# A hybrid encoder on one core: the first pair of up tiles as eight plain half products, with its combinations of activations made during it

## The chip, the core and the metric

The kernel runs on one core of a Trainium2 chip. The core has five engines with a queue of instructions each: PE (TensorE) multiplies matrices, DVE (VectorE), ACT (ScalarE) and POOL (GpSimd) work element by element, SP (SyncE) here issues nearly all DMAs. They run side by side and wait for each other by semaphores. PE's results go to PSUM, which this kernel uses as eight banks of 128 x 512 f32 values; the tiles named below lie in SBUF, the other on-chip memory.

The metric is the device time of one execution in microseconds (us). A run gives one such time; the median of several runs is compared.

## The reference, cut to what matters

One encoder layer is applied to 1024 prompt tokens and 256 sample tokens. The part that the change touches is the end of the cross-attention and the beginning of the feed-forward network:

```python
x = x + memory_cross_attention(rmsnorm(x, norm_xa_w), rmsnorm(mem, norm_mem_w), xa_w_q, xa_w_kv, xa_w_o)
h = rmsnorm(x, norm_ffn_w)
gu = h @ ffn_w_gate_up
x = x + (jax.nn.silu(gu[..., :D_FF]) * gu[..., D_FF:]) @ ffn_w_down
```

D_MODEL is 1024 and D_FF is 2816, so h @ ffn_w_gate_up has 22 gate tiles and 22 up tiles of 128 columns. Tile f of each belong together: silu(gate) * up is one row block of the input of the down product.

## The kernel before

**Precision.** Every f32 operand x of a matrix product is split into two parts, hi (x rounded by a copy on ACT) and lo = x - hi (on DVE or POOL), and a product is three matmuls: hi by hi, lo by hi, hi by lo (`mm3`). `split` makes both parts, and its lo part always has the line L126, the hi part L125. All matmuls of PE that matter here have the line L108.

**Tiling.** Activations lie transposed: 128 partitions of the model dimension, tokens along the free axis, eight such tiles (k = 0 to 7) for 1024. The tokens are in three blocks: x0 (prompt, 512), x1 (prompt, 512) and x2 (sample, 256). A weight tile has 128 x 1024 values: eight k pieces of 128 x 128.

**The up stage** (`ff_first`, `ff_up`, driven by `up`) runs over f = 0 to 21, one gate tile and one up tile per f; here such an f is called a pair. For the prompt, the pair's gate and up tile (two columns of blocks) by the two halves of the model dimension (k 0 to 3 and k 4 to 7) by the two token blocks are a 2 x 2 by 2 x 2 block product, done with seven half products rather than eight, each of 4 k pieces, 12 matmuls of 512 columns. It needs sums of the weight tiles (`gu_sa`, `gu_sb`, on POOL, in the tile `room`) and combinations of the activations, which are made once: b11 and b21 are the two halves of x0's normed activations, b12 and b22 those of x1's, r1 = b11 - b12, r2 = b22 - r1 (up to sign), t3 = b22 - b12, t4 from r2 and b21. r1 lies in the place of b12. The sample's products are plain (`sample`): 24 matmuls of 256 columns each for gate and up.

**Before it** the output projection of the attention (`OutProj.run`) computes x0, x1, x2 (evacuated by DVE, L1230) and starts three norms (`Norm.rest`) as side jobs: x0's, x1's and the sample's. A norm sums squares, has a step on PE (matmul of nacc by a column of ones), a chain of eleven short DVE instructions (L258, L224, L226 to L228) for the inverse root nst, a second step on PE (nst by the identity), then for each k a multiplication on DVE (L276) and a split. In the kernel before, x1's norm makes r1 in x0 (L1422) and r2 in four banks of PSUM (`r2_raw`, L1426) as it goes; `make_t3` (L1559) and `make_t4` (L1568) follow in `ff_first` between the seven products of the first pair.

**What sets the order.** PE's order is the order in which the Python code emits its instructions: the main generator (`K.main`) emits products, and after each one the side jobs whose time has come by an estimated clock (`K.clock`, `pump`) emit theirs; LAGS, LAGS2 and PACE1 are such delays. The order on the other engines is made by a scheduler when the program is built. Each engine then executes its queue strictly in order. PSUM's banks are two pools of four: pm for the products of the main generator, pq (`bank()`) for the norms, sums and the sample.

**Loads.** `gu_load` loads the pair f's two weight tiles by SP, alternately into two places; `gu_gate`, `gu_sa`, `gu_sb`, `gu_up` split them, with the lo parts mostly on POOL. For the first pair, `first_weights` and `after` do so during the output projection. Results of the up stage go to DRAM (gq for the prompt's combinations, gsd for the sample); the down stage after it is not touched.

Of the kernel before, what the change touches and what calls it, by code (L numbers as in the profile page):

```python
# [163 lines left out]
def trunk_kernel(ctx: ExitStack, tc: tile.TileContext, a):  # L164
# [52 lines left out]
    def bank(p=pq, tag="b"):  # L217
        return p.tile([P, 512], F32, tag=tag, name="bank")
# [1195 lines left out]
    def sinks(b, x, hs):  # L1414
        hi, lo = hs[b]
        x0, x1 = x[0], x[1]
        if b == 0:
            return lambda k, t: split(hi[:, k, :], lo[:, k, :], t, V if k % 2 else G)

        def sink(k, t):  # L1420
            if k < 4:
                V.tensor_tensor(out=x0[:, k, :], in0=x0[:, k, :], in1=t, op=ALU.subtract)  # L1422
                split(hi[:, k, :], lo[:, k, :], x0[:, k, :], V)
            else:
                r2_raw.append(bank())
                V.scalar_tensor_tensor(out=r2_raw[k - 4], in0=t, scalar=-1.0, in1=x0[:, k - 4, :], op0=ALU.mult, op1=ALU.subtract)  # L1426
# [6 lines left out]
    r2_raw = []  # L1433
    first_out = []

    def copies_read():

        if not first_out:
            return False
        h3[2] = h3[2][0], hp.tile([P, KT, NS], F32R, tag="lo2", name="lo2")  # L1440
        return True
# [48 lines left out]
    def first_weights():  # L1490

        gu_load(0, wp)

        def sums():
            yield FIRST_W
            g, u = gu_raw[0]
            hi, lo = gu_w[0, 1] = pair_of(wp)
            s2, s1 = bank(), bank()
            V.tensor_tensor(out=s1, in0=u[:, :512], in1=u[:, 512:], op=ALU.add)
            V.tensor_tensor(out=s2, in0=s1, in1=g[:, :512], op=ALU.add)  # L1500
            gu_gate(0)
            split(hi[:, :512], lo[:, :512], s2)
            split(hi[:, 512:], lo[:, 512:], s1)
            yield 3000
            V.tensor_tensor(out=g[:, :512], in0=g[:, :512], in1=u[:, :512], op=ALU.add)
            V.tensor_tensor(out=g[:, 512:], in0=s2, in1=g[:, 512:], op=ALU.add)

        K.side(sums())
# [30 lines left out]
    def parts(hl, k, src, eng):  # L1539
        split(hl[0][:, k, :], hl[1][:, k, :], src, eng)  # L1540

    def r2_ready():
        for k in range(4):
            parts(r2, k, r2_raw[k], V)

    K.main(op.run(x1d, 1.0, S_FFN, x2p, x2d, sinks, first_weights, copies_read, after))
    x0, x1 = op.x[0], op.x[1]
    K.finish(K.pending.pop((id(h3), 1)))
# [3 lines left out]
    first_copies = hp.tile([P, 4, 512], F32, tag="lo2", name="copies")  # L1552
    split(*gu_w[0, 3], gu_raw[0][1], G)
    fs = ExitStack()
    t4 = []

    def make_t3():
        for k in range(4):
            V.tensor_tensor(out=x1[:, k, :], in0=x1[:, k + 4, :], in1=x1[:, k, :], op=ALU.subtract)  # L1559
            parts(t3, k, x1[:, k, :], V)  # L1560
        xhs.close()

    def make_t4():
        nonlocal fp
        fp = fs.enter_context(pool("ffn", side="right"))
        t4.extend(fp.tile([P, 4, 512], F32R, tag=f"t4{i}", name=f"t4{i}") for i in "hl")
        for k in range(4):
            V.scalar_tensor_tensor(out=x0[:, k + 4, :], in0=r2_raw[k], scalar=-1.0, in1=x0[:, k + 4, :], op0=ALU.mult, op1=ALU.subtract)  # L1568
            parts(t4, k, x0[:, k + 4, :], V)

    def make_room():
        nonlocal room
        room = x0p.tile([P, KT, 512], F32, tag="x0", name="room")

    fp = room = None
# [153 lines left out]
    def ff_first():  # L1729


        w = lambda i: gu_w[0, i]
        pb, pf, pe, pa = (bank(pm) for _ in range(4))
        cs = first_copies
        gu_load(1, wp)
        yield from gu_mm(pb, w(0), 1, b21, True)
        yield from gu_mm(pa, w(0), 0, b11, True)
        p1 = copied(pa, cs[:, 0, :])
        t1 = gate_of(pb, p1)
        yield from gu_mm(pe, w(1), 1, r1, True)  # L1740
        make_t3()
        yield from gu_mm(pa, w(1), 0, r2, False)
        gu_gate(1, V)
        yield from gu_mm(pf, w(2), 1, b22, True)
        u2 = copied(pa, cs[:, 1, :])
        V.tensor_tensor(out=u2, in0=u2, in1=pe, op=ALU.add)
        t2 = gate_of(pf, u2)
        make_t4()
        make_room()
        yield from gu_mm(pa, w(2), 0, t3, False)  # L1750
        c22 = copied(pa, second_block(0))
        V.tensor_tensor(out=c22, in0=c22, in1=pe, op=ALU.add)
        times_up(t2, c22, store2(0), -1.0, c22)
        pn = bank(pm)
        yield from gu_mm(pn, gu_w[1, 0], 0, b11, True)
        yield from gu_mm(pa, w(3), 1, t4, False)
        times_up(t1, pa, store1(0), -1.0)
        pending["last"] = 0, t1, c22
        pn2 = bank(pm)
        first_out.extend((pn, pn2))  # L1760
        yield from gu_mm(pn2, gu_w[1, 0], 1, b21, True)

    def ff_up(f):
        w = lambda i: gu_w[f, i]
        second, last = f == 1, f == NFF - 1
        sums = lambda: (bank()[:, :NS], bank()[:, :NS])
        if second:
            pa, pb = first_out
            p1 = copied(pa)
            t1 = gate_of(pb, p1)  # L1770
            combine(*pending["last"])
            K.finish(K.pending.pop((id(h3), 2)))
            smp.extend(half(h3[2], i) for i in range(2))
            sg0, su0 = sums()
            yield from sample(sg0, gu_w[0, 0], (0, 1))
            gu_sa(1)
            ts0 = silu2(sg0, NS)
            sg, su = sums()
            yield from sample(su0, gu_w[0, 3], (0, 1))
            times_up(ts0, su0, gsd[0], 1.0)  # L1780
        else:
            pa, pb = bank(pm), bank(pm)
            yield from gu_mm(pa, w(0), 0, b11, True)
            p1 = copied(pa)
            sg, su = sums()
            yield from sample(sg, w(0), (0,))
            yield from gu_mm(pb, w(0), 1, b21, True)
            t1 = gate_of(pb, p1)
            combine(*pending["last"])
        gu_sb(f)  # L1790
        gu_load(f + 1, wp if f % 2 == 0 else x2p)
        yield from sample(sg, w(0), (0, 1) if second else (1,))
        yield from gu_mm(pa, w(1), 0, r2, False)
        u2 = copied(pa)
        gu_up(f)
# [9 lines left out]
        yield from sample(su, w(3), (0, 1))  # L1805
# [248 lines left out]
LAGS, LAGS2, FIRST_W = 11000, 9000, 9000  # L2054
PACE1 = 1900
# [82 lines left out]
```

## Time and profile before

| | us |
|---|---|
| median of 3 runs | 2257.51 |
| all runs | 2257.51, 2257.01, 2261.9 |
| span of the profiled execution | 2255.3 |
| busy in it: PE / DVE / ACT / POOL | 2197.5 / 1394.5 / 816.5 / 536.0 |
| the up stage in it begins | 1396.98 |

The profiled execution is another one than those timed, and its own time is known by its span, from the first to the last instruction; what lies around it is the difference to a run's time, some 2 us against the median.

How to read the views that follow: a line of the timeline has the start, the duration, the engine, the line of the kernel, the operation, its output and input by the program's names, the shape, and a count where equal instructions follow each other; in brackets stands how long the engine was idle before it and what ended that. Matmuls overlap in the pipeline, so the step from start to start is the price of one, and not its duration. In a view of windows the columns are the window, its length, the busy time of PE, PE's weight loads, DVE, ACT and POOL (with counts), then the granted clock of PE, the busy share of the DMA engines and GB/s. Line numbers (L1568) are those of the kernel printed above.

### The profile page before, as it was taken

The numbers are of one execution on the slowest core, as the hardware profiler recorded it, in microseconds if no ns is written. First come the engines' busy times: TensorE is split into PE (matmuls) and PEld (weight loads), VectorE is DVE, ScalarE is ACT, GpSimd is POOL, SyncE is SP. The second block draws the span as 40 slices with busy tenths as digits, with TensorE's granted clock in tenths as the row PEclk, the third lists the DMA queues.
The fourth block names the chain that finished last, engine by engine and source line by source line (L and its number), as shares of the span: only waits on it lengthen the run. The fifth ranks groups of instructions, "written<-read, shape, count | busy, mean of one in ns | idle before, by whom it ended". The sixth has DMA issues, their size and how long they took to land.

```text
span 2255.3 us, 32407 instructions
## 1 busy us (share of the span) xinstructions
PE 2197.5 (97%) x12464; PEld 1919.1 (85%) x12464; DVE 1394.5 (62%) x2765; ACT 816.5 (36%) x1480; POOL 536.0 (24%) x361
## 2 busy tenths in 40 slices
PE   6999999999999999999999998999999999999998
PEld 6988888888888898788888887888888888878888
DVE  7768788887985964664533547543443344468575
ACT  5434243433424433232344423332323232343453
POOL 3010000000000000013221332656665666100031
PEclk9999999999999999999999999999999999999999
DMA  5222322323234445962231432222222222493531
GB/s 186 83 79 68 104 69 87 79 66 95 73 115 121 159 142 166 310 226 94 91 101 43 164 135 74 81 90 84 83 84 79 78 86 96 152 338 108 201 108 57
DMA packets 191302, 262.48 MB, mean 116 GB/s; under 512 B 72410, under 2 KB 102698, under 8 KB 191146
## 3 DMA queue, kind: packets, MB, share of 16 engines
q1 hardware_dynamic: 171306, 231.30, 30.5%
q10 hardware_dynamic: 19840, 29.11, 3.5%
q8 instruction: 98, 1.61, 0.3%
q14 instruction: 58, 0.48, 0.1%
HBM read 182.19 MB, written 78.16 MB: 115 GB/s over the span
## 4 chain that ended last, share of the span: by engine, by line
PE 83%; DVE 8%; issue 4%; DMA 3%; ACT 2%; POOL 0%; SPq 0%; POOLq 0%; ACTq 0%; DVEq 0%
PE bank L108 82%; DMA tbd<-stage 1%; PE bank L121 1%; DVE acc L591 1%; DVE wlo L126 1%; DMA braw<-gq 1%; DVE nt L276 1%; DVE lo L126 0%; DVE sw L895 0%; DVE U L837 0%; DMA t<-sgd 0%; DVE nacc L244 0%; DVE aT L706 0%; ACT acc L589 0%; ACT whi L125 0%
## 5 line engine op out<-in xcount | busy, mean ns | idle before, releaser
L108 PE MATMUL bank<-hi,whi 128*128 128x512 f32 (+1 forms) x2144 | 762.8, 356 | 0.0
L108 PE MATMUL bank<-lo,whi 128*128 128x512 f32 (+1 forms) x2144 | 748.1, 349 | 0.0
L108 PE MATMUL bank<-hi,wlo 128*128 128x512 f32 (+1 forms) x2144 | 747.8, 349 | 0.0
L108 PEld LDWEIGHTS bank<-hi,wlo 128*128 128x128 f32 x2144 | 405.4, 189 | 53.9
L108 PEld LDWEIGHTS bank<-hi,whi 128*128 128x128 f32 x2144 | 406.2, 189 | 49.4 <-issue 0.2
L108 PEld LDWEIGHTS bank<-lo,whi 128*128 128x128 f32 x2144 | 406.4, 190 | 48.4 <-issue 0.2
L126 POOL TENSOR_TENSOR wlo<-raw,whi 128x1024 fp32r<-128x1024 f32 x72 | 174.0, 2418 | 467.2 <-ACT whi L125 467.2
L125 ACT ACTIVATE whi<-raw 128x1024 fp32r<-128x1024 f32 (+1 forms) x135 | 140.5, 1042 | 241.0 <-PE bank L108 182.7
L108 PE MATMUL bank<-bhl,whi 128*128 128x512 f32 x456 | 140.5, 389 | 0.0
L126 POOL TENSOR_TENSOR wlo<-room,whi 128x1024 fp32r<-128x1024 f32 x42 | 100.8, 2401 | 51.9 <-ACT whi L125 50.8
L108 PEld LDWEIGHTS bank<-bhl,whi 128*128 128x128 f32 x456 | 85.5, 188 | 17.8
L126 DVE TENSOR_TENSOR wlo<-raw,whi 128x1024 fp32r<-128x1024 f32 (+1 forms) x63 | 75.4, 1197 | 31.3 <-ACT whi L125 28.7
L1802 DVE TENSOR_TENSOR room<-room,bank 128x512 f32<-128x512 f32 x21 | 14.5, 688 | 127.0 <-ACT room L1588 127.0
L108 PE MATMUL bank<-bhl,wlo 128*128 128x512 f32 x228 | 88.8, 390 | 1.7 <-DVE wlo L126 1.7
L591 DVE SCALAR_TENSOR_TENSOR acc<-craw,sm,acc 128x510 f32<-128x510 f32 (+1 forms) x96 | 73.6, 766 | 20.5 <-ACT acc L589 19.0
L244 POOL TENSOR_TENSOR nacc<-nacc,nsq 128x512 f32<-128x512 f32 (+1 forms) x21 | 27.4, 1306 | 237.1 <-ACT nsq L243 213.0
L1601 DVE SCALAR_TENSOR_TENSOR t<-t,room 128x512 f32<-128x512 f32 x42 | 64.9, 1546 | 29.6 <-ACT t L1600 29.6
L737 DVE TENSOR_TENSOR W<-W,UT 128x2 f32<-128x2 f32 (+30 forms) x155 | 73.1, 472 | 9.9 <-DMA W<-in_eye 5.6
L243 ACT ACTIVATE nsq<-x 128x512 f32<-128x512 f32 (+1 forms) x70 | 40.0, 583 | 101.1 <-DVE x L1230 93.0
L954 ACT ACTIVATE gs<-bank 128x512 f32<-128x512 f32 (+1 forms) x60 | 31.2, 520 | 125.2 <-PE bank L108 119.9
L1610 DVE SCALAR_TENSOR_TENSOR t<-bank,t 128x512 f32<-128x512 f32 (+1 forms) x44 | 24.5, 558 | 81.5 <-PE bank L108 81.5
L1230 DVE SCALAR_TENSOR_TENSOR x<-bank,x 128x512 f32<-128x512 f32 (+1 forms) x48 | 28.6, 599 | 74.0 <-PE bank L108 65.6
(334 smaller groups left out, 4270.5 us busy)
## 6 DMA issues: line engine op xcount, KB each, us to landing
raw<-in_w_gu SPq DMA_DIRECT2D x44, 512.0 KB, 3.2
braw<-gq SPq DMA_DIRECT2D x14, 1024.0 KB, 5.5
raw<-in_w_g SPq DMA_DIRECT2D x20, 512.0 KB, 3.3
gq<-t SPq DMA_DIRECT2D x33, 256.0 KB, 2.0
gtd<-gs ACTq DMA_DIRECT2D x32, 256.0 KB, 2.0
w<-in_w_dn SPq DMA_DIRECT2D x8, 1024.0 KB, 8.8
raw<-in_w_qkv SPq DMA_DIRECT2D x12, 512.0 KB, 3.5
gq<-r SPq DMA_DIRECT2D x22, 256.0 KB, 2.0
```

What stands on the lines that cost most here:

```text
L108: self.nc.tensor.matmul(out, l, r, start=start, stop=stop, skip_group_check=more)
L121: self.nc.tensor.transpose(out, x, ident)
L125: self.nc.scalar.activation(hi, src, AF.Copy)
L126: (eng or self.nc.vector).tensor_tensor(out=lo, in0=src, in1=f32(hi), op=ALU.subtract)
L243: S.activation(sq, x, AF.Square)
L244: (eng or V).tensor_tensor(out=self.acc, in0=self.acc, in1=sq, op=ALU.add)
L591: V.scalar_tensor_tensor(out=dst, in0=src, scalar=wj, in1=dst, op0=ALU.mult, op1=ALU.add)
L737: V.tensor_tensor(out=t3, in0=u3[:, i:, c:].rearrange("p j c -> p c j"), in1=XL[:, 32 * i + i : 32 * i + 32].unsqueeze(1).to_broadcast([P, ...
L954: S.activation(t, ps, AF.Tanh, scale=0.5)
L1230: V.scalar_tensor_tensor(out=x[b][:, m, :], in0=ps, scalar=scale, in1=x[b][:, m, :], op0=ALU.mult, op1=ALU.add)
L1601: V.scalar_tensor_tensor(out=t, in0=t, scalar=1.0, in1=src, op0=ALU.add, op1=ALU.mult)
L1610: V.scalar_tensor_tensor(out=out, in0=u, scalar=sign, in1=t, op0=ALU.mult, op1=ALU.mult)
```

## The change

The first pair is no longer done by seven half products but by eight plain ones: gate and up tile, each by both halves, for both token blocks (`ff_first`). The products with b12 come before those with b22, because r1 is written over b12 as soon as the former are done (`b12_read`). The combinations r1, r2, t3, t4 are made by a side job (`combinations`) that starts when x1's norm is emitted, in place in x0 and x1 and in pieces 1024 wide instead of 512; no bank of PSUM holds r2 and no tile `copies` is used any more. The sums of the first pair's weights (`sums` in `first_weights`) go; both its tiles are split on POOL in `after`. The sample's products of the first pair stand at the end of `ff_first`, and in the second pair (`second`) the sample's up product stands before the r2 product. `room` is x0's tile itself, whose pieces are free once the combinations are split. LAGS, LAGS2 and PACE1 have other values; COMB is a delay of the new side job. From the third pair on the code is as before.

```diff
     def sinks(b, x, hs):
         hi, lo = hs[b]
-        x0, x1 = x[0], x[1]
-        if b == 0:
-            return lambda k, t: split(hi[:, k, :], lo[:, k, :], t, V if k % 2 else G)
-
-        def sink(k, t):
-            if k < 4:
-                V.tensor_tensor(out=x0[:, k, :], in0=x0[:, k, :], in1=t, op=ALU.subtract)
-                split(hi[:, k, :], lo[:, k, :], x0[:, k, :], V)
-            else:
-                r2_raw.append(bank())
-                V.scalar_tensor_tensor(out=r2_raw[k - 4], in0=t, scalar=-1.0, in1=x0[:, k - 4, :], op0=ALU.mult, op1=ALU.subtract)
-                split(hi[:, k, :], lo[:, k, :], t, V)
-                if k == KT - 1:
-                    r2_ready()
-
-        return sink
+        return lambda k, t: split(hi[:, k, :], lo[:, k, :], t, V if b or k % 2 else G)
...
     def first_weights():
         gu_load(0, wp)
-        def sums():
-            yield FIRST_W
...
     def after(m):
-        if m == 2:
-            gu_w[0, 2] = room_of()
-            split(*gu_w[0, 2], gu_raw[0][0], G)
-        elif m == 7:
-            gu_w[0, 3] = room_of()
-        else:
-            for x, t in zip(r2 if m < 5 else t3, room_of()):
+        if m in (2, 3):
+            gu_w[0, m] = room_of()
+            split(*gu_w[0, m], gu_raw[0][m - 2], G)
+        elif m > 3:
+            for x, t in zip(r2 if m < 6 else t3, room_of()):
                 x.parts.append(t.rearrange("p (k t) -> p k t", t=512))
...
+    def combinations():
+
+        normed = K.pending[id(h3), 1]
+        while normed in K.sides:
+            yield 300
+        at = lambda x, i: x[:, i : i + 2, :]
+
+        def two(dst, src, x, i):
+            split(at(dst[0], i), at(dst[1], i), at(src, x + i), V)
+
+        for i in (0, 2):
+            V.tensor_tensor(out=at(x0, i), in0=at(x0, i), in1=at(x1, i), op=ALU.subtract)
+        yield COMB
+        for i in (0, 2):
+            V.tensor_tensor(out=at(x1, i), in0=at(x1, i + 4), in1=at(x1, i), op=ALU.subtract)
+        yield COMB
+        for i in (0, 2):
+            V.scalar_tensor_tensor(out=at(x1, i + 4), in0=at(x1, i + 4), scalar=-1.0, in1=at(x0, i), op0=ALU.mult, op1=ALU.subtract)
+        yield COMB
+        for i in (0, 2):
+            V.scalar_tensor_tensor(out=at(x0, i + 4), in0=at(x1, i + 4), scalar=-1.0, in1=at(x0, i + 4), op0=ALU.mult, op1=ALU.subtract)
+        yield COMB
+        for dst, x in ((r2, 4), (t3, 0)):
+            for i in (0, 2):
+                split(*(d.parts[i // 2] for d in dst), at(x1, x + i), V)
+            yield COMB
         xhs.close()
...
+        while not b12_read:
+            yield 300
+        for i in (0, 2):
+            two(r1, x0, 0, i)
+        yield COMB
+        for i in (0, 2):
+            two(t4, x0, 4, i)
...
     def ff_first():
...
+        yield from block(g0, wg, ((0, b11), (1, b21)))
+        t1 = silu2(g0)
+        yield from block(u0, wu, ((0, b11), (1, b21)))
+        times_up(t1, u0, store1(0), 1.0)
+        K.finish(K.pending.pop((id(h3), 1)))
+        yield from block(g1, wg, ((0, r1),))
+        yield from block(u1, wu, ((0, r1),))
+        b12_read.append(0)
+        yield from block(g1, wg, ((1, b22),))
+        t2 = silu2(g1)
+        c22 = ff(x2p, "nacc", "c22", bufs=2)
+        yield from block(u1, wu, ((1, b22),))
+        times_up(t2, u1, store2(0), 1.0, c22)
         pending["last"] = 0, t1, c22
...
+        K.finish(K.pending.pop((id(h3), 2)))
+        smp.extend(half(h3[2], i) for i in range(2))
+        sg, su = bank()[:, :NS], bank()[:, :NS]
+        yield from sample(sg, wg, (0, 1))
+        ts = silu2(sg, NS)
+        K.finish(made)
+        gu_sa(1)
+        yield from sample(su, wu, (0, 1))
+        times_up(ts, su, gsd[0], 1.0)
...
-LAGS, LAGS2, FIRST_W = 11000, 9000, 9000
-PACE1 = 1900
+LAGS, LAGS2, COMB = 4000, 7000, 1500
+PACE1 = 1500
```

More of the change, by code (lines that the diff above doesn't have):

```diff
@@ L1729, in ff_first @@
     def ff_first():
-        w = lambda i: gu_w[0, i]
-        pb, pf, pe, pa = (bank(pm) for _ in range(4))
-        cs = first_copies
+        wg, wu = gu_w[0, 2], gu_w[0, 3]
+        made = K.side(combinations())
+        g0, g1, u0, u1 = (bank(pm) for _ in range(4))
         gu_load(1, wp)
[L1736 to L1740, printed above, removed]
@@ L1804, in ff_up @@
         ts_ = silu2(sg, NS)
-        yield from sample(su, w(3), (0, 1))
+        if not second:
+            yield from sample(su, w(3), (0, 1))
         times_up(ts_, su, gsd[f], 1.0)
```

108 lines of the change are left out of this document (21 added, 87 removed).

## The prediction

> **What bounds the kernel now.** First the page: span and busy shares, then who waits for whom on PE, then the chain of waits.
>
> ```profile
> span 2255.3 us, 32407 instructions
> PE 2197.5 (97%) x12464; PEld 1919.1 (85%) x12464; DVE 1394.5 (62%) x2765; ACT 816.5 (36%) x1480; POOL 536.0 (24%) x361
> ```
> ```profile
> PE bank L108 <- DVE nacc L244: 11.8, 5, 9.0
> PE bank L108 <- DVE x L1568: 8.0, 1, 8.0
> ```
>
> PE sets the time. Its single long wait after the start (the 9.0 us one is at the start) is for L1568, a line that the change deletes. The chain of waits, first around this wait, then over the whole run, shows what precedes and follows it:
>
> ```profile
> 1402.71 0.61 DVE bank L1426
> ...
> 1403.92 2.39 DVE wlo L126 x4
> ...
> 1411.26 0.61 DVE x L1568
> 1411.88 0.14 issue
> ```
> ```profile
> 1412.01 533.94 PE bank L108 x2821
> ```
>
> Up to 1412 the chain is a row of DVE instructions without a gap; from there to 1946 it is PE alone. So a microsecond saved or added on PE in the up stage counts fully. The timeline of PE gives the paces and the loss:
>
> ```profile
> 1396.98 0.40 PE L108 MATMUL bank<-hi,whi 128*128 128x512 f32 x1
> ...
> 1403.58 0.39 PE L108 MATMUL bank<-hi,wlo 128*128 128x512 f32 x1
> 1412.01 0.99 PE L108 MATMUL bank<-cst,nacc 128*128 128x1 f32 x4 [8.05 <-DVE x L1568]
> 1412.86 0.77 PE L108 MATMUL bank<-hi,whi 128*128 128x512 f32 x1
> ```
> ```profile
> 1433.37 0.28 PE L108 MATMUL bank<-hi,whi 128*128 128x256 f32 x1
> ...
> 1442.01 0.40 PE L108 MATMUL bank<-whi 128*128 128x512 f32 x1
> ...
> 1457.24 0.39 PE L108 MATMUL bank<-hi,whi 128*128 128x512 f32 x1
> ...
> 1459.28 0.39 PE L108 MATMUL bank<-hi,whi 128*128 128x512 f32 x1
> ```
> ```profile
> 1380.03 1.02 PE L108 MATMUL bank<-cst,nacc 128*128 128x1 f32 x8 [0.18 <-DVE nacc L244]
> 1380.91 0.36 PE L108 MATMUL bank<-hi,whi 128*128 128x256 f32 x1
> ...
> 1425.33 0.61 PE L108 MATMUL bank<-cst,nst 128*128 128x128 f32 x4
> 1425.69 0.48 PE L108 MATMUL bank<-hi,whi 128*128 128x512 f32 x1
> ```
>
> From start to start, nine 512-column matmuls take 1459.28 - 1457.24 = 2.04 us, 0.227 each; 72 of 256 columns take 1442.01 - 1433.37 = 8.64, 0.12 each (the durations overlap and are no price). From 1396.98, where the up stage begins, to 1442.01, the built order has 108 of the first, 72 of the second and the sample's two norm steps (half of 0.88, since it has four matmuls for eight, and 0.36 us): 24.5 + 8.6 + 0.8 = 33.9 us of 45.0. So **11.1 us are lost there**, 8.05 idle and 3.0 slow. Why slow, the windows of one microsecond tell (column after POOL: granted clock):
>
> ```profile
> 1407.00:1408.00 1.00, 0.00 (x0) 0.00 (x0) 1.00 (x2) 0.94 (x2) 0.10 (x1) 0.62 0.00 0
> ...
> 1416.00:1417.00 1.00, 1.00 (x4) 0.81 (x3) 1.00 (x3) 0.44 (x1) 0.00 (x0) 0.50 0.00 0
> 1417.00:1418.00 1.00, 1.00 (x5) 0.82 (x4) 1.00 (x5) 0.82 (x2) 0.00 (x0) 0.76 0.00 0
> ```
>
> The clock falls some 3.3 us into the idle time, is 0.50 in between, and is back 5.5 us after PE restarts.
>
> **The change, part by part.** *Removed:* the wait. The sample's norm step (L108 on cst,nacc) needed a bank of PSUM, and r2_raw held all four until make_t4 (L1568) read one. Now the combinations stay in the x tiles. That gives back 11.1 us.
>
> *Added:* 8 products for 7, twelve 512-column matmuls: 12 x 0.227 = 2.7 us on PE. The rest of PE's work is the same, moved about. The first pair's weight sums (five DVE instructions, L1499 to L1506 and their splits) go, and POOL splits the up tile as it does the gate tile; that lay between 1350 and 1390, where PE had no wait, and is worth nothing. On SP the second pair's second load now stands ahead of the sample's x2d store and not behind it; it is issued as soon as POOL frees its tile, near 1389, and is needed 40 us later: nothing either. If these covers were gone, each would cost one split, 1 to 2.4 us.
>
> *Moved:* on DVE, the work that was spread over the first norm and the products now stands behind the first norm, in 1024-wide instructions, and the sample's second norm step is threaded through it. x_12577 and x_12578 are the prompt's two x tiles (x0, x1), nst the inverse root. DVE before, at the wait:
>
> ```order
> L1559 TENSOR_TENSOR x_12578<-x_12578 128x512 x2
> L1568 SCALAR_TENSOR_TENSOR x_12577<-bank,x_12577 128x512
> L126 TENSOR_TENSOR wlo<-x_12578,whi 128x512
> L258 TENSOR_SCALAR bank<-bank 128x2
> L126 TENSOR_TENSOR wlo<-x_12578,whi 128x512
> L224 TENSOR_SCALAR nst<-bank 128x2
> ```
>
> and in the changed kernel (with its own line numbers), at the same norm's end:
>
> ```order
> L1524 SCALAR_TENSOR_TENSOR x_12577<-x_12578,x_12577 128x1024
> L226 SCALAR_TENSOR_TENSOR bank<-nst,bank 128x2
> L126 TENSOR_TENSOR wlo<-x_12578,whi 128x1024
> L227 TENSOR_TENSOR bank<-bank,nst 128x2
> L126 TENSOR_TENSOR wlo<-x_12578,whi 128x1024
> L228 SCALAR_TENSOR_TENSOR nst<-bank,nst 128x2
> L1574 SCALAR_TENSOR_TENSOR t<-bank,t 128x512
> L226 SCALAR_TENSOR_TENSOR bank<-nst,bank 128x2
> L126 TENSOR_TENSOR wlo<-x_12578,whi 128x1024
> L227 TENSOR_TENSOR bank<-bank,nst 128x2
> L126 TENSOR_TENSOR wlo<-x_12578,whi 128x1024
> L228 SCALAR_TENSOR_TENSOR nst<-bank,nst 128x2
> ```
>
> Each short step now has a 1024-wide instruction ahead of it, and PE's cst,nst step, which stands after 9 matmuls of the third product, waits for the last row. In PE's order of the changed kernel (hi_12891 is the prompt's second block):
>
> ```order
> L108 MATMUL bank<-hi_12891,whi 128x512
> L108 MATMUL bank<-lo_12892,whi 128x512
> L108 MATMUL bank<-hi_12891,wlo 128x512
> L108 MATMUL bank<-cst,nst 128x128 x2
> L108 MATMUL bank<-hi_12891,whi 128x512
> ```
>
> All products behind it wait too. When does DVE get there? Its prices, from its timeline (starts again):
>
> ```profile
> 1388.89 1.28 DVE L126 TENSOR_TENSOR lo<-x,hi 128x512 fp32r<-128x512 f32 x2
> 1390.10 0.73 DVE L276 SCALAR_TENSOR_TENSOR x<-x,sm,bank 128x512 f32<-128x512 f32 x1
> ...
> 1397.68 0.42 DVE L1230 SCALAR_TENSOR_TENSOR x<-bank,x 128x256 f32<-128x256 f32 x1
> 1398.01 1.04 DVE L1426 SCALAR_TENSOR_TENSOR bank<-x,x 128x512 f32<-128x512 f32 x1
> ...
> 1413.11 0.68 DVE L126 TENSOR_TENSOR wlo<-x,whi 128x512 fp32r<-128x512 f32 x1
> 1413.71 0.15 DVE L224 TENSOR_SCALAR nst<-bank 128x2 int32<-128x2 int32 x1
> 1413.78 0.69 DVE L1568 SCALAR_TENSOR_TENSOR x<-bank,x 128x512 f32<-128x512 f32 x1
> ```
> ```profile
> 1997.05 2.35 DVE L126 TENSOR_TENSOR bhl<-braw,bhl 128x1024 fp32r<-128x1024 f32 x2
> 1999.32 1.22 DVE L126 TENSOR_TENSOR ahl<-w,ahl 128x1024 fp32r<-128x1024 f32 x1
> ```
>
> A 512-wide one costs 0.61, a 1024-wide one (1999.32 - 1997.05) / 2 = 1.14, a short norm step 0.07, L1230 0.33. No row has a 1024-wide SCALAR_TENSOR_TENSOR; at 512 both kinds take about 0.6, so 1.14 again, and at most 2 x 0.61. DVE cannot begin before L1230 of the last product of the output projection, which PE ends at 1396.98 as before; so 1397.2. In the built order there follow, through the last row above: L1230, thirteen 1024-wide (one weight split, eight combinations, four splits), five 512-wide, eleven short: 0.33 + 14.8 + 3.05 + 0.8 = 19.0, so 1416.2, and PE goes on 0.14 later (the "issue" row): **1416.35**. PE is there after 48 + 9 matmuls and the first norm step: 1396.98 + 57 x 0.227 + 0.44 = 1410.4. **A new wait of 5.9 us** (5.1 if the short steps cost nothing, 7.0 if every 1024-wide one costs 1.22), DVE again its end. ACT's halves of these splits (1.0 each, below) follow their combinations and are ahead of DVE's.
>
> The clock after it: the wait before cost 3.0 us of slow matmuls. The one other place of this kind in the windows is 1976 to 1980:
>
> ```profile
> 1972.00:1976.00 4.00, 1.55 (x7) 0.72 (x5) 3.48 (x4) 3.33 (x4) 0.00 (x0) 1.00 1.01 389
> 1976.00:1980.00 4.00, 2.90 (x8) 2.24 (x8) 1.16 (x2) 0.00 (x0) 0.00 (x0) 0.66 0.79 251
> ```
>
> There 3.55 us of idle time in two pieces sufficed to halve it, for about 3.4 us, costing some 1.7. I take 2.2, between the two, bounds 0.5 and 3.4.
>
> [...]
>
> *The sample, now last.* Its split needs x_12579 on DVE and POOL, where the sums of the next weights (L1447, L1448, L1457, L1458) now go into x0's room and so stand behind the late combinations. POOL before (lo_13573 is the sample's low half) and now (lo_12894):
>
> ```order
> L1472 TENSOR_TENSOR room<-raw 128x512
> L1482 TENSOR_TENSOR room<-raw 128x512
> L1473 TENSOR_TENSOR room<-room,raw 128x512
> L1483 TENSOR_TENSOR room<-room,raw 128x512
> L126 TENSOR_TENSOR wlo<-room,whi 128x1024
> L126 TENSOR_TENSOR lo_13573<-x_12579,hi_12893 128x256 x4
> ```
> ```order
> L126 TENSOR_TENSOR lo_12894<-x_12579,hi_12893 128x256 x3
> L1457 TENSOR_TENSOR x_12577<-raw 128x512
> L126 TENSOR_TENSOR lo_12894<-x_12579,hi_12893 128x256
> L1447 TENSOR_TENSOR x_12577<-raw 128x512
> L1448 TENSOR_TENSOR x_12577<-x_12577,raw 128x512
> L1458 TENSOR_TENSOR x_12577<-x_12577,raw 128x512
> L126 TENSOR_TENSOR wlo<-x_12577,whi 128x1024 x2
> L1447 TENSOR_TENSOR x_12577<-raw 128x512
> L126 TENSOR_TENSOR wlo<-raw,whi 128x1024
> ```
>
> The sums moved behind three of the sample's four splits, and the split of the second up tile (last row) behind a sum for the pair after. DVE and POOL then work at once, and the timelines of both show that they take turns where both inputs lie in SBUF:
>
> ```profile
> 1419.91 1.29 POOL L1482 TENSOR_TENSOR room<-raw 128x512 f32<-128x512 f32 x1
> 1421.17 2.28 POOL L1473 TENSOR_TENSOR room<-room,raw 128x512 f32<-128x512 f32 x1
> 1430.74 1.62 POOL L126 TENSOR_TENSOR lo<-x,hi 128x256 fp32r<-128x256 f32 x2 [1.20 <-ACT hi L125]
> ```
> ```profile
> 1420.27 2.01 DVE L126 TENSOR_TENSOR wlo<-raw,whi 128x1024 fp32r<-128x1024 f32 x1 [1.62 <-ACT whi L125]
> ```
> ```profile
> 1424.85 1.06 ACT L125 ACTIVATE whi<-room 128x1024 fp32r<-128x1024 f32 x1 [0.38 <-POOL room L1483]
> ```
>
> DVE's 1.14 became 2.01 and POOL's second sum 2.28 for 1.29. Let E be the end of the last product that reads b12 (its place is then written with r1): the restart at 1416.35, the norm step 0.36, 15 matmuls 3.4 and the slow clock 2.2, so 1422.3. From E: ACT 1.2 (the 1.06 and its start), DVE 1.15, then in turns POOL 0.8, DVE 0.4, POOL 1.29, DVE 1.15, POOL 0.8, DVE 1.15, POOL 1.29, DVE 0.4: the sample's last low half is ready at E + 9.6. PE wants it after 24 matmuls and 22 of the sample's, E + 8.1: **1.6 us** of waiting (without turns E + 5.9, so 0; two more POOL turns, 3.5). The sample's up product of the second pair, moved forward, needs the second tile's split at E + 21.4; POOL's list gives E + 21.4 to 22.2, so **0.5** (0 to 2). From there on PE's order is as before, and the chain's row of 533.94 us shows it without waits.
>
> *Sum:* 2.7 - 11.1 + 5.9 + 2.2 + 1.6 + 0.5 = +1.8 us on the span of 2255.3. The median of the runs is 2257.5, 2.2 above that span; the same offset gives **2259.3**. With all bounds low, 2.7 - 11.1 + 5.1 + 0.5 = -2.8; with all high, +7.5 (7.0, 3.4, 3.5, 2.0), which I don't expect together.
>
> **Rivals.** *A: the new wait does not come.* If DVE reached the norm step by 1410.4, only 2.7 - 11.1 + 0.5 would be left, -7.9: 2249.6. For it: the waits in front are gone, and 1024-wide instructions save 0.07 each. Against: thirteen of them need 14.8 us in a stretch of 13.2. *B: POOL's list decides, slower.* The second tile's split stands behind a sum whose load SP issues only after a store of the first pair's combination and after a load that waits for L1458. If POOL and DVE lose two more turns, the sample waits 3.5 and the up product 3: 1.8 + 1.9 + 2.5 = +6.2, 2263.7. It decides once the two waits together exceed 4.8 us (2.1 and the 2.7 that are left to +4.5). For it: 1.29 to 2.28 above; against: POOL has nothing to do for 20 us ahead. *C: the clock stays up* through 5.9 us: +1.8 - 2.2 = -0.4, 2257.1; the row at 1976 is against it. [...]
>
> **How the numbers follow.** Forecast 0.58, A 0.12, B 0.18, C 0.12. A measurement of this kernel tells 0.2%, 4.5 us, from no change: A is faster (0.12), B slower (0.18), the forecast and C within (0.70). The forecast's own range is 2255 to 2262; with B and part of the way to A, 2253.5 to 2264.
>
> **What would show it.** In the changed profile: no wait of PE at the sample's first norm step (cst,nacc); a wait for nst L228 of 5 to 7 us near 1410, with the granted clock at 0.5 behind it; a short wait for the sample's lo near 1430; the up tiles from the second pair on at 0.227 per matmul. Wrong it would be if nst is done by 1411 (A), or if waits for wlo of the second pair exceed 2 us (B).

## The result and the profile after

The changed kernel takes 2264.77 us (median of 14 runs, 2261.79 to 2268.01); the kernel before, run alternately with it, 2259.11 us (14 runs, 2255.91 to 2262.91). The ratio is 1.0024, 95% interval 1.0017 to 1.0032: 5.4 us slower, above the predicted range, and slower where no change was the likeliest case.

The page of the changed kernel, its span and its busy times, and the list of what PE waited for between 1390 and 1480 us (us in total, times, longest):

```profile
span 2262.5 us, 32394 instructions
PE 2201.9 (97%) x12476; PEld 1922.1 (85%) x12476; DVE 1392.5 (62%) x2743; ACT 813.0 (36%) x1470; POOL 538.2 (24%) x360
```
```profile
PE bank L108 <- DVE nst L228: 6.3, 1, 6.3
PE bank L108 <- POOL wlo L126: 2.8, 1, 2.8
PE bank L108 <- ACT x L1552: 0.7, 1, 0.7
```

The 8.0 us for L1568 are gone and three waits stand in their place. PE's timeline (start, duration; in brackets the idle time ahead and what ended it), with the first 512-column matmul of the up stage and the first matmul of the stage behind it:

```profile
1396.95 0.40 PE L108 MATMUL bank<-hi,whi 128*128 128x512 f32 x1
...
1416.82 1.19 PE L108 MATMUL bank<-cst,nst 128*128 128x128 f32 x4 [6.26 <-DVE nst L228]
...
1445.82 0.58 PE L108 MATMUL bank<-hi,wlo 128*128 128x256 f32 x1 [2.77 <-POOL wlo L126]
...
1459.02 0.50 PE L108 MATMUL bank<-t4h,whi 128*128 128x512 f32 x1 [0.69 <-ACT x L1552]
...
1963.19 0.62 PE L108 MATMUL bank<-bhl,whi 128*128 128x512 f32 x2
```

From the first of these rows to the last are 566.24 us. In the kernel before the same two places are 1396.98 (quoted with the prediction) and this:

```profile
1957.13 0.61 PE L108 MATMUL bank<-bhl,whi 128*128 128x512 f32 x2
```

That is 560.15 us, so **the stage has grown by 6.1 us**. This interval, called the up stage below, does not contain what differs from one execution to the next ahead of it: the stage began between 1396.1 and 1402.1 in the profiled executions of this study, though the program up to there is the same in the change and all its variants.

The windows of one microsecond (the column after POOL is the granted clock) show two cold stretches, one at each of the two longer waits:

```profile
1414.00:1415.00 1.00, 0.00 (x0) 0.00 (x0) 1.00 (x3) 0.00 (x0) 0.00 (x0) 0.97 0.00 0
...
1420.00:1421.00 1.00, 1.00 (x4) 0.81 (x3) 1.00 (x4) 0.97 (x3) 0.96 (x2) 0.50 0.00 0
1421.00:1422.00 1.00, 1.00 (x4) 0.76 (x4) 1.00 (x3) 0.11 (x1) 0.48 (x1) 0.61 0.00 0
...
1445.00:1446.00 1.00, 0.18 (x1) 0.19 (x2) 0.00 (x0) 0.00 (x0) 1.00 (x2) 0.83 0.00 0
...
1448.00:1449.00 1.00, 1.00 (x7) 1.00 (x7) 0.00 (x0) 0.00 (x0) 1.00 (x2) 0.50 0.40 160
1449.00:1450.00 1.00, 1.00 (x10) 1.00 (x10) 0.00 (x0) 0.00 (x0) 1.00 (x2) 0.96 0.00 0
```

At 0.50 a 512-column matmul took 0.43 us from start to start (1418.66 to 1419.09, and so to 1421.2) where it took 0.227 at 1.00, so time at 0.50 is counted as half lost: 4.2 us at 0.50 and one at 0.61 behind the first wait are 2.5 us, 3.2 us at 0.50 behind the second are 1.6. The account of the stage is then +2.7 (the twelve matmuls) - 11.1 (the old wait and its cold clock) + 6.3 + 2.5 + 2.8 + 1.6 + 0.7 = +5.5, of 6.1 measured. The 2.7 is the prediction's price, which no run measured by itself, and 0.6 us are left over.

The second wait is the one that the prediction had at 0.5. The chain of waits, from the start of the stage:

```profile
1397.15 0.42 DVE x L1230
...
1408.80 1.12 DVE x L1524
...
1416.60 0.08 DVE nst L228
...
1416.82 5.04 PE bank L108 x13
...
1429.01 1.43 DVE lo L126
...
1431.95 1.60 DVE r L1588
...
1434.35 7.21 DMA raw<-in_w_gu
...
1445.82 12.53 PE bank L108 x58
```

and POOL's timeline beside it, with SP's issues of the loads:

```profile
1431.69 1.30 POOL L1458 TENSOR_TENSOR x<-x,raw 128x512 f32<-128x512 f32 x1
1432.95 5.22 POOL L126 TENSOR_TENSOR wlo<-x,whi 128x1024 fp32r<-128x1024 f32 x2
1441.70 1.29 POOL L1447 TENSOR_TENSOR x<-raw 128x512 f32<-128x512 f32 x1 [3.52 <-DMA raw<-in_w_gu]
1442.95 2.81 POOL L126 TENSOR_TENSOR wlo<-raw,whi 128x1024 fp32r<-128x1024 f32 x1
```
```profile
1433.02 0.80 SPq L1428 DMA_DIRECT2D raw<-in_w_gu  x2
1433.92 0.38 SPq L1589 DMA_DIRECT2D gq<-r  x1
1434.35 0.42 SPq L1428 DMA_DIRECT2D raw<-in_w_gu  x1
```

Read from below: the split that PE needs (wlo<-raw, 1442.95) stands on POOL behind L1447, a sum for the pair after. PE does not need that sum yet, but its load has not landed. On SP's queue a load had waited 18.4 us for L1458 to free its place; behind it stand another load, the store of r (made by L1588) and the load of this sum. So three loads of 512 KB and a store go out within 1.4 us, and the third load lands 7.2 us after its issue, where these loads took 3.2 us (median) in the kernel before. POOL stands idle for 3.52 us with the split's own data at hand (ACT had made its hi part by 1435.4).

One run of e9 below, 2425.54 us at a mean granted clock of 0.848 where all others had 0.991 to 0.996, is left out of its figures.

### The profile page after: what moved, and what is told of

Its sections match the earlier page's. It is cut to its first block, busy times and chain, and to the rows that moved or that the text cites. A ratio compares the mean times of both kernels' runs of the same rounds, so it can differ in the third digit from the quotient of the medians.

```text
span 2262.5 us, 32394 instructions
## 1 busy us (share of the span) xinstructions
PE 2201.9 (97%) x12476; PEld 1922.1 (85%) x12476; DVE 1392.5 (62%) x2743; ACT 813.0 (36%) x1470; POOL 538.2 (24%) x360
## 4 chain that ended last, share of the span: by engine, by line
PE 79%; DVE 10%; issue 4%; DMA 4%; ACT 2%; POOL 0%; SPq 0%; ACTq 0%; POOLq 0%; DVEq 0%
PE bank L108 78%; DMA tbd<-stage 1%; PE bank L121 1%; DVE wlo L126 1%; DVE acc L591 1%; DVE W L737 1%; DVE lo L126 1%; DMA t<-sgd 1%; DVE nt L276 0%; DVE sw L895 0%; DVE W L740 0%; DMA braw<-gq 0%; DMA x<-x2d 0%; DVE U L837 0%; DVE nacc L244 0%
## 5 line engine op out<-in xcount | busy, mean ns | idle before, releaser
L126 POOL TENSOR_TENSOR wlo<-x,whi 128x1024 fp32r<-128x1024 f32 x42 | 101.2, 2411 | 51.6 <-ACT whi L125 51.6
L1758 DVE TENSOR_TENSOR x<-x,bank 128x512 f32<-128x512 f32 x21 | 14.5, 689 | 128.2 <-ACT x L1552 128.2
L1565 DVE SCALAR_TENSOR_TENSOR t<-t,x 128x512 f32<-128x512 f32 x42 | 64.9, 1545 | 29.8 <-ACT t L1564 29.8
L125 ACT ACTIVATE whi<-x 128x1024 fp32r<-128x1024 f32 x46 | 48.6, 1061 | 80.0 <-PE bank L108 71.8
```

What stands on the lines that cost most here:

```text
L125: self.nc.scalar.activation(hi, src, AF.Copy)
L126: (eng or self.nc.vector).tensor_tensor(out=lo, in0=src, in1=f32(hi), op=ALU.subtract)
L1565: V.scalar_tensor_tensor(out=t, in0=t, scalar=1.0, in1=src, op0=ALU.add, op1=ALU.mult)
```

## The experiments

e1 to e4, e5 to e8 and e9 to e11 are three sets, each timed in five rounds together with the kernel before on one chip. The table gives the ratio with its 95% interval, and the up stage against that of the kernel before (560.15 us). The stage is that of one profiled execution, the ratio that of all: taken both in us, the two columns differ by up to 2.3 us, to either side.

| kernel | ratio to before | up stage |
|---|---|---|
| the change | 1.0024 [1.0017, 1.0032] | +6.1 |
| e1, second pair's sample product back | 1.0000 [0.9991, 1.0009] | +1.1 |
| e2, second up split on DVE | 1.0011 [1.0001, 1.0020] | +1.1 |
| e3, nst step 30 matmuls later | 1.0020 [1.0011, 1.0030] | +4.9 |
| e4, twelve more matmuls | 1.0027 [1.0017, 1.0037] | +4.8 |
| e5, first norm step 15 matmuls earlier | 1.0003 [0.9995, 1.0012] | +0.1 |
| e6, e5 and e1 | 0.9998 [0.9989, 1.0007] | -2.3 |
| e7, e6 and four splits on POOL | 1.0008 [0.9999, 1.0016] | +2.9 |
| e8, before with the first norm step later | 1.0006 [0.9997, 1.0015] | +0.6 |
| e9, e6 and two products ahead of the sample | 1.0013 [1.0003, 1.0024] | +2.4 |
| e10, e9 and the nst step 6 matmuls later | 0.9975 [0.9966, 0.9984] | -4.5 |
| e11, e6 again | 1.0000 [0.9991, 1.0009] | -2.3 |

**e1 and e2: is it the second pair's split?** e1 puts the reader back, e2 moves the split to another engine.

```diff
-        if second:
-            yield from sample(su, w(3), (0, 1))
         yield from gu_mm(pa, w(1), 0, r2, False)
...
-        if not second:
-            yield from sample(su, w(3), (0, 1))
+        yield from sample(su, w(3), (0, 1))
```
```diff
-        split(*gu_w[f, 3], gu_raw[f][1], G)
+        split(*gu_w[f, 3], gu_raw[f][1], V if f == 1 else G)
```

> The second pair's sample product with the up tile goes back to where it stood before the change (behind t3's product, ahead of t4's), nothing else. Theory (the loss is four separate waits): PE no longer reaches the second up tile at 1443 but some 11 us later, so the 2.8 us wait for wlo, the 1.6 us of half clock behind it and the 0.7 us wait of t4's product for ACT's copy go: 5.1 us less than the changed kernel, span near 2257.4, while the 6.3 us wait for nst stays as it is. Rival (POOL's list is late as a whole and any reader of these tiles will wait): a wait of 2 us or more turns up at another tile of the second pair and less than 2 us is won. Rival (the 12 extra matmuls and wider instructions are the loss): nothing changes.

> The low half of the second pair's up tile is made by DVE instead of POOL, nothing else; PE's order stays that of the changed kernel. Theory (the split is late only because it stands on POOL behind a sum whose load landed late): the 2.8 us wait and its 1.6 us of half clock go, the 0.7 us wait of t4's product stays: 4.4 us less than the changed kernel, span near 2258.1. The late load itself (7.2 us) stays and hits nobody. Rival (the tile's own inputs or its buffer are late): DVE waits at this split and PE's wait stays, 0 to 1 us won.

The waits of PE in e1, in the same stretch, are down to one row, and POOL's late sum stands there as before and hurts nobody:

```profile
PE bank L108 <- DVE nst L228: 6.3, 1, 6.3
```
```profile
1441.17 1.30 POOL L1447 TENSOR_TENSOR x<-raw 128x512 f32<-128x512 f32 x1 [3.47 <-DMA raw<-in_w_gu]
```

In e2, POOL's sum waits for its load too, and the split is made on DVE, ahead of it:

```profile
1443.46 1.30 POOL L1447 TENSOR_TENSOR x<-raw 128x512 f32<-128x512 f32 x1 [2.55 <-DMA raw<-in_w_gu]
```
```profile
1437.20 1.45 DVE L126 TENSOR_TENSOR wlo<-raw,whi 128x1024 fp32r<-128x1024 f32 x1
```

Each gives back 5.0 us of the stage (5.1 and 4.4 expected; the half microsecond more in e2 is a shorter cold stretch behind the nst wait). By the ratios e1 gives back 5.4 us and e2 2.9, each known to some 2.7 us. Neither the twelve matmuls nor the nst wait was touched. So 4.4 of the 6.1 us are POOL's order at one place with the clock behind it, 0.7 the wait of t4's product for ACT, and the rest of the change, the first pair, costs about 1.1.

**e3: is the wait for nst a matter of its place?** `LAGS2` 7000 to 13000.

> The sample's second norm step (matmuls on cst,nst) stands 30 matmuls later in PE's order, 6.8 us, so that PE has products to do while DVE finishes nst. Theory (DVE's list bounds the stretch up to the sample's product, PE only waits at one place or another): the 6.3 us wait at this step goes, and a wait of about as much stands at the sample's own product for its low halves, since DVE and POOL cannot start on them before nst is done near 1416.5: the total within 2 us of the changed kernel. Rival (the wait is made only by the place of the step in PE's order): 6.3 + 2.5 = 8.8 us less, span near 2253.7.

The waits of e3:

```profile
1427.38 0.58 PE L108 MATMUL bank<-hi,whi 128*128 128x256 f32 x1 [6.47 <-ACT hi L125]
1430.50 0.58 PE L108 MATMUL bank<-lo,whi 128*128 128x256 f32 x1 [2.54 <-POOL lo L126]
```

6.26 us went at the norm step and 9.0 came at the sample's product, where the 256-wide halves are read; the wait for the up tile's split went too, since PE came later and POOL's order there changed. In all -1.2 us: the wait moved, and the total is as the theory had it. But DVE's list was not all that held the sample up, as rows of DVE, ACT and POOL show:

```profile
1427.66 2.19 DVE L126 TENSOR_TENSOR lo<-x,hi 128x256 fp32r<-128x256 f32 x1 [3.26 <-ACT hi L125]
```
```profile
1425.96 1.06 ACT L125 ACTIVATE whi<-x 128x1024 fp32r<-128x1024 f32 x1 [5.67 <-POOL x L1448]
```
```profile
1418.91 4.45 POOL L1457 TENSOR_TENSOR x<-raw 128x512 f32<-128x512 f32 x1 [18.58 <-DVE lo L126]
```

nst was done at 1417.6. With the step moved, the sums of the second pair's weights stand ahead of the sample's halves on POOL, and on ACT the copy of such a sum stands ahead of the sample's copies. The first row of these sums, L1457, took 4.45 us beside DVE's splits, ACT waited for L1448 behind it, and DVE stood idle for 3.26 us until ACT came. So e3 shows that a wait moves with its step; that DVE's list alone bounds the stretch up to the sample it does not show.

**e4: are matmuls ahead of the wait free?**

```diff
+        yield from gu_mm(g0, wg, 0, b11, True)
         yield from block(g0, wg, ((0, b11), (1, b21)))
-LAGS, LAGS2, COMB = 4000, 7000, 1500
+LAGS, LAGS2, COMB = 6560, 7000, 1500
```

> Twelve 512-column matmuls more at the front of the first product (their sum is overwritten, the result is the same), and the sample's norm step as many products later in time. Theory (PE waits for DVE behind them anyway): the wait for nst gets 2.7 us shorter, so they cost nothing: -1 to +0.5 us against the changed kernel, and so the change's own twelve extra matmuls cost nothing either. Rival (as my prediction summed it, every matmul counts on PE): +2.7 us.

The wait for nst is 5.1 us, 1.2 shorter and not 2.7, since with the first norm step DVE's short steps came later as well; the wait for the split fell from 2.8 to 1.1 and had no cold clock behind it. The stage is 1.3 us shorter, the ratio 0.0003 higher with an interval of 0.001 to each side. The sum decides for neither theory: the wait for the split alone brought 3.3 us (1.7, and 1.6 of half clock), and without it the stage would be 2.0 us longer, where the matmuls' 2.7 less the 1.2 are 1.5. Since two terms moved at once, what a matmul costs there is not settled by it.

**e5 and e6: fewer rows ahead of nst.** `LAGS, LAGS2` from 4000, 7000 to 1000, 10000; e6 adds the edit of e1.

> The sample's first norm step (cst,nacc) stands 15 matmuls earlier in PE's order, its second one (cst,nst) where it stood; nothing else. DVE's short steps then begin some 5 us earlier, and three 1024-wide instructions and one of 512 fewer stand ahead of the last of them: nst 3 x 1.14 + 0.6 = 4.0 to 4.5 us earlier. Theory (those rows ahead of nst are the wait): the wait for nst falls from 6.3 to about 2 us, too short to halve the clock, so 4.3 + 2.5 = 6.8 us are won there, and up to 1.9 us of it are given back at the sample's product, whose low halves come only 4.3 us earlier: 4.9 to 6.8 us less than the changed kernel, span 2255.7 to 2257.6; the 2.8 us wait for wlo stays. Rival (DVE's total work up to the sample is the bound, wherever nst stands): the sample's product waits for all of it, 0 to 2 us won.

> Both edits at once: the sample's first norm step 15 matmuls earlier, and the second pair's sample product with the up tile back behind t3's product. Theory (separate waits add): 4.9 to 6.8 of the one and 5.0 of the other, 9.9 to 11.8 us less than the changed kernel, which is 4.5 to 6 us less than the kernel before. Rival (they share one bound, DVE's and POOL's late lists): no more than 7 us less than the changed kernel.

PE's waits in e5 and in e6:

```profile
1416.33 0.68 PE L108 MATMUL bank<-cst,nst 128*128 128x128 f32 x4 [1.85 <-DVE nst L228]
1428.79 0.38 PE L108 MATMUL bank<-hi,whi 128*128 128x256 f32 x1 [0.40 <-ACT hi L125]
1431.58 0.39 PE L108 MATMUL bank<-lo,whi 128*128 128x256 f32 x1 [2.40 <-DVE lo L126]
```
```profile
1414.20 0.68 PE L108 MATMUL bank<-cst,nst 128*128 128x128 f32 x4 [1.83 <-DVE nst L228]
...
1429.45 0.38 PE L108 MATMUL bank<-lo,whi 128*128 128x256 f32 x1 [2.40 <-DVE lo L126]
```

The step to 1.85 us came as worked out: nst was done 4.0 us earlier in the stage, so the rows ahead of it on DVE were the wait. That a wait of about 2 us is too short to halve the clock, as was expected, no run shows: the clock stayed at 1.00 behind the 1.85 us here, fell to 0.50 behind the 2.40, and fell behind 1.83 us in e9. At the sample more was given back than the up to 1.9 expected, 2.8 us of waits and some 1.6 of half clock. But e5 won 6.0 us in spite of that, because the wait for the up tile's split was gone as well, which had been expected to stay: with the sample's halves earlier, the built order has that split ahead of L1447, and the sum's wait stands behind it:

```profile
1439.58 2.86 POOL L126 TENSOR_TENSOR wlo<-raw,whi 128x1024 fp32r<-128x1024 f32 x1
1443.46 1.29 POOL L1447 TENSOR_TENSOR x<-raw 128x512 f32<-128x512 f32 x1 [1.03 <-DMA raw<-in_w_gu]
```

So e6 had little left to win with the edit of e1: 8.4 us of the stage against the change and not 9.9 to 11.8, and by the ratios 5.9, within the rival's 7. Of the 2.4 us between e5 and e6, 0.7 is the wait of t4's product and some 1.6 the half clock at the sample, which e6 did not have behind the same waits. The gains did not add, since both edits remove the same wait. The runs of e6 and e11, twice the same kernel, are equal to the kernel before (0.9998, 1.0000), though the stage is 2.3 us shorter in their profiled executions; the clock, below, may be why, but no run shows it.

**e7: the splits of r2 and t3 on POOL.**

```diff
-                split(*(d.parts[i // 2] for d in dst), at(x1, x + i), V)
+                split(*(d.parts[i // 2] for d in dst), at(x1, x + i), G)
```

> As the run with both edits, and the four 1024-wide low halves of r2 and t3 go from DVE to POOL, which is idle there. DVE then has one 1024-wide row fewer ahead of nst, and three fewer behind it. Theory (two engines that read SBUF at once take turns, so the work is only shared, and POOL's sample halves then stand behind four splits of 2.4 us): nst 1 us earlier, the sample's low halves not, total within 2 us of the run with both edits. Rival (DVE's row count is all that matters): the wait for nst is gone and the sample's product waits no more, 2 to 4 us less than the run with both edits.

Both expectations missed: the stage is 5.2 us longer than in e6. The wait for nst went from 1.8 to 3.4 us, and DVE's timeline has the reason, one row of two alike beside POOL's first split:

```profile
1408.14 1.21 DVE L1524 SCALAR_TENSOR_TENSOR x<-x,x 128x1024 f32<-128x1024 f32 x1
...
1409.34 3.33 DVE L1524 SCALAR_TENSOR_TENSOR x<-x,x 128x1024 f32<-128x1024 f32 x1
```
```profile
1408.12 11.49 POOL L126 TENSOR_TENSOR wlo<-x,whi 128x1024 fp32r<-128x1024 f32 x4 [9.66 <-PE bank L108]
```

The second L1524 took 3.33 us where the first took 1.21. POOL's first split, beside both, took 3.46 (such a split takes 2.4 alone) and ended at 1411.58, and this L1524 1.1 us later. It stands ahead of the last short steps, so nst, with fewer rows ahead of it, came later. So this L1524 ended its own time (1.21) after POOL's split, and the split was as much longer as the first L1524 lasts: in these rows the two engines took turns. The kernel before has it too: between 1440 and 1940 us the 512-wide L1601, with both inputs in SBUF, took 2.48 us each of the 20 times that POOL was at work when it began and 0.69 without POOL, and L1605, with one input from a bank, 0.69 and 0.68. Of the 5.2 us, 2.6 are longer waits (for nst and at the sample), and some 2.9 the half clock behind the sample's wait of 3.5 us, which e6 did not have.

**e8: the old wait by itself.** The kernel before with `LAGS` 16000 for 11000.

> The kernel before, with the sample's first norm step (cst,nacc) 24 matmuls later in PE's order, 5.4 us; nothing else. It tells what the old wait of 8.05 us for L1568 and its 3.0 us of slow matmuls were worth by themselves. Theory (PE waits there only because the step stands ahead of products that it could do): the wait falls to about 2.6 us, the clock stays up, 8 us less than the kernel before, ratio near 0.9963. Rival (DVE's list bounds that stretch too): PE waits for the splits of t3 or t4 at a product instead, total within 2 us of the kernel before.

```profile
1415.17 0.98 PE L108 MATMUL bank<-cst,nacc 128*128 128x1 f32 x4 [6.24 <-DVE x L1568]
```

The rival's time came true, its place did not: PE still waits for L1568. That row let PE go 1415.17 - 1396.50 = 18.7 us after the start of the stage, where it was 15.0 before, because DVE's order changed with the step, and 1.8 us of waits came at the sample. That speaks for DVE's list as the bound in the kernel before, too, and for PE's wait for a bank as only the place where it showed; no run moved the step with DVE's order kept.

**e9 to e11: a faster version, and the mechanism once more.** e9 puts the second pair's first two half products ahead of the first pair's sample; e10 has `LAGS2` 11500 besides.

```diff
+        K.finish(made)
+        pa, pb = bank(pm), bank(pm)
+        first_out.extend((pa, pb))
+        yield from gu_mm(pa, gu_w[1, 0], 0, b11, True)
+        yield from gu_mm(pb, gu_w[1, 0], 1, b21, True)
         K.finish(K.pending.pop((id(h3), 2)))
...
-        K.finish(made)
         gu_sa(1)
...
-        pa, pb = bank(pm), bank(pm)
-        yield from gu_mm(pa, w(0), 0, b11, True)
+        pa, pb = first_out if second else (bank(pm), bank(pm))
+        if not second:
+            yield from gu_mm(pa, w(0), 0, b11, True)
```

> As the run with both edits (norm step early, second pair's sample product back), and the second pair's first two half products, which need nothing of the sample, now stand ahead of the first pair's sample products, so that PE has 24 matmuls, 5.4 us, more to do while DVE and POOL finish the sample's halves. Theory (PE waits at the sample because the sample stands first of what is left; the rest is not bound by DVE): the waits of 0.4 and 2.4 us at the sample go, no slow clock can follow them, the 1.8 us wait for nst stays: 2.8 us less than the run with both edits where that kept the clock, 4.5 less where it did not. Rival (DVE's and POOL's lists bound the second pair's sums as well): the wait reappears at the second pair's w1 or w2, 0 to 1 us won.

> As the run before in this list, and the sample's second norm step six matmuls later in PE's order, 1.36 us. Theory: with 5.4 us of products now behind it, the wait for nst falls from 1.8 to 0.5 us and nothing gets it back: 1.3 us less. Rival (the sample's halves come later by as much and PE waits for them, as it did when this step was moved by 30 matmuls): no difference.

> The run with both edits once more, unchanged. In the two runs before, the same waits (1.8 for nst, 0.4 and 2.4 us at the sample, in the same order of work) were followed by 3 us of half clock in the one and by none in the other. [...] Rival (the kernel's own order decides): no half clock again.

e9 was to be faster than e6 and is slower by 4.7 us of the stage. The sample's waits are gone, as the theory had it, but PE waits 1.16 and 3.23 us for wlo, 1.6 us more than at the sample in e6, and the clock was halved for 3.4 us behind the nst wait and as long again behind the last, 3.4 us lost in all. By the ratios e9 is 3.4 us slower than e6. Its runs go with the clock: three at a mean granted clock of 0.992, the profiled one among them, took 2264.4 to 2266.2 us, and seven at 0.994 to 0.996 2256.9 to 2260.7. POOL's timeline of e9, and then of e10:

```profile
1446.33 1.28 POOL L1447 TENSOR_TENSOR x<-raw 128x512 f32<-128x512 f32 x1 [6.07 <-DMA raw<-in_w_gu]
1447.58 2.37 POOL L126 TENSOR_TENSOR wlo<-x,whi 128x1024 fp32r<-128x1024 f32 x1
```
```profile
1434.86 5.95 POOL L126 TENSOR_TENSOR wlo<-x,whi 128x1024 fp32r<-128x1024 f32 x2
1443.34 1.29 POOL L1447 TENSOR_TENSOR x<-raw 128x512 f32<-128x512 f32 x1 [2.53 <-DMA raw<-in_w_gu]
```

In e9 the sum stands between the second pair's two splits and holds the later one up for 6.07 us; in e10 both splits are ahead of it, and its idle time delays only the up tile's split, by 0.9 us for PE. Six matmuls' difference in the place of the norm step turned the order on POOL, and the stage is 6.9 us shorter. Of these, the order on POOL is 3.5 (0.9 us of waits for wlo where there were 4.4) and the half clock, which e10 did not have, 3.4. The theory of e10 had 1.3: the wait for nst did fall to 0.5, and 1.2 us came back at the sample, as the rival had it. e10 is the best version here: 0.9975 of the kernel before, 2252.72 us in the median.

## Why the prediction was wrong

**What bounds the kernel.** Right for PE, and for DVE up to nst: with fewer rows ahead of it, in e5, nst came 4.0 us earlier, as worked out. From there to the sample's product POOL and ACT can hold PE as well (e3).

**The old wait, -11.1.** Right: no row for L1568 is left, and PE did not wait at the cst,nacc step.

**The new wait, 5.9.** Right in place, cause and size: 6.26 us for nst L228, DVE without a gap from 1397.15 to 1416.6, its 1024-wide rows at 1.12 to 1.14 each, the SCALAR_TENSOR_TENSOR of L1524 at 1.12. Rival A (no wait) fell.

**The cold clock, 2.2.** Right: 2.5. Rival C (clock stays up) fell.

**The twelve matmuls, 2.7.** Never seen alone. The account closes with them to 0.6 us, and e1, which differs from the kernel before by the first pair, stands at +1.1, where the prediction's terms for that pair give 2.7 - 11.1 + 5.9 + 2.2 + 1.6 = +1.3. That they meet is luck in part, since the 1.6 did not come. e4 could not separate them.

**The sample's low halves, 1.6.** It was 0: by the chain E is 1421.86 and the last of them was done at 1430.44, E + 8.6 where 9.6 was counted. PE wanted it at 1431.16, E + 9.3 where 8.1 was counted, since it had 29 of the 512-column matmuls behind E and not 24.

**The second up tile's split, 0.5 (0 to 2).** This is the step that failed: "POOL's list gives E + 21.4 to 22.2, so 0.5". PE came at E + 21.2 (PE would have been there at 1445.82 - 2.77 = 1443.05); the split was done at E + 23.9. POOL's work was summed as rows by durations, and the load of the sum in between was taken to be there. It landed at 1441.6. The text named the place under rival B, "a sum whose load SP issues only after a store", and priced it by POOL's and DVE's turns; the price was the load, 3.52 us of idle POOL. The sum had no cold clock behind this wait either, and there were 1.6 us of it. With the 4.4 us for this term that the profile shows, less its 0.5, and without the sample's 1.6, the sum would have been +4.1, so about 2261.6.

**Rival B, slower, 0.18.** Its sign came, a wait for wlo of the second pair above 2 us (2.77), and so did its place. Its +6.2 lies close to the 6.1 of the stage by luck: it had 1.9 us more at the sample, which did not come, and neither the cold clock nor the wait of t4's product.

**From there on "without waits".** Wrong by 0.7: moving the sample's up product away left t4's product directly behind t3's, and PE waits for ACT to copy the bank between them. e1 has no such wait.

**The offset.** The prediction went from a median of 2257.51 over three runs; in the set with the changed kernel the kernel before had 2259.11. That moves the time by 1.6, the ratio by nothing. The range of 2253.5 to 2264 would reach 2265.6 from that median, so it missed 2264.77 by this offset; the forecast of +1.8 for +5.4 is as far off from either.

## What to carry to other kernels

On an engine that issues in order, an instruction for later work is as dangerous as its latest input: when a step is moved, look at each queue for what now stands ahead of its inputs, and price that by when its DMA is issued and lands, not by its duration alone (here 3.52 us of idle POOL ahead of a sum of 1.29). A wait moves when the waiting step is moved, and the new order on the other engines can make it longer (9.0 us for 6.3 in e3); shortening the list ahead of it wins (e5, 1.85 us for 6.26). When two edits each win several microseconds, ask whether they remove the same wait before adding them (e6).

## What the runs showed of the hardware

**A wait of 1.8 us can be followed by half clock, and one of 3.4 need not be.** The waits of e5 and e6 above are the same to 0.02 us (the middle one of e6, 0.41, is not shown). In e5 the clock was halved behind the last, in e6 and e11 it stayed at 1.00 throughout. In e7 it stayed at 1.00 behind this wait:

```profile
1413.54 0.68 PE L108 MATMUL bank<-cst,nst 128*128 128x128 f32 x4 [3.41 <-DVE nst L228]
```

In e9 the first wait alone, 1.83 us, had this behind it, PE at full work:

```profile
1418.00:1419.00 1.00, 1.00 (x7) 0.86 (x7) 1.00 (x2) 0.00 (x0) 0.00 (x0) 1.00 0.00 0
1419.00:1420.00 1.00, 1.00 (x4) 0.73 (x3) 1.00 (x3) 0.34 (x1) 0.00 (x0) 0.50 0.00 0
...
1422.00:1423.00 1.00, 1.00 (x5) 0.78 (x5) 1.00 (x4) 0.61 (x1) 0.49 (x1) 0.79 0.00 0
```

The drop came 1.4 us after PE had resumed and lasted 3.4 us (a mean of 0.79 in the last window is 0.42 us at half). The other cold stretches have the same length or a multiple of it: 3.4 us behind the second wait of the change (from 1445.66 to 1449.08, by the means 0.83 and 0.96), 6.8 us from within its first (from 1414.94 to 1421.78, by the means 0.97 and 0.61), and 10.2 us in the kernel before (from 1407.24 to 1417.48, by 0.62 and 0.76). Why equal waits end differently, and how long PE must stand idle before the clock falls, no run shows: none varied a wait by itself, so it stays open.

**The third of three loads issued together landed late.** A 512 KB load of these weights took 3.2 us (median) in the kernel before, and 7.2 us in the change as the third of three issued within 1.4 us, with a store among them. With no store among them the third took 7.6 us in e10, where the three went out within 1.4 us, and 6.4 in e9, within 1.8. No run spaced them by itself: that the company is the reason was not tested.
